# Second input phase: product P1 of the last two blocks as seven inner products, with written engine orders

## The chip, the cores and the metric

The program runs on one core of a Trainium2 chip. The metric is device time in microseconds (us) of one execution. The engines are PE (TensorE: matmuls, with their weight loads shown as PEld), DVE (VectorE), ACT (ScalarE), POOL (GpSimd) and SP (SyncE, which here only issues DMAs). Each engine works through its own list of instructions in a fixed order; waits between engines go by semaphores.

## The reference

With one layer, only the pooling mixer and the norms count:

```
h = x + pool_mixer(rms_norm(x, norm_w))          # x: (1, 4096, 1024) float32
out = rms_norm(h, final_norm_w)

def pool_mixer(h, in_w, group_w, group_b, scale, out_w):
    u, gate = split(h @ in_w, 2)                 # in_w: (1024, 2048)
    ug = u in 4 groups of 256 channels
    pooled = trailing_mean(ug[g], window 2/4/8/16) - ug
    mixed = einsum(pooled, group_w) + group_b    # 256 x 256 for each group
    return (mixed * scale * silu(gate)) @ out_w  # out_w: (1024, 1024)
```

The result must be close to float32: every float32 factor is split into a high and a low part, and each product is done as three matmul passes (high by high, high by low, low by high).

## The kernel before

**Stages.** The 4096 tokens go through three stages, in `steps`. Stage "a" (four blocks of 1024 tokens, numbered 0 to 3) makes the channels of groups 0 and 1, stage "b" (the same four blocks) those of groups 2 and 3, and stage "o" (eight blocks of 512 tokens) the output projection. The linear map of each group is folded into `in_w` at the start, so that a stage's product has 1024 output columns: 512 to be pooled and 512 of the gate.

**Seven products.** Each block's product is done as seven products of half size (Strassen's scheme in Winograd's form), P1 to P7, run in the order P1, P2, P7, P6, P5, P4, P3 (`ORDER_IN`). One such product is 48 matmuls of 512 columns. It writes four PSUM banks: P1 and P2 the banks 0 to 3 (set "x"), P7 and P4 the same banks (set "v"), P6, P5 and P3 the banks 4 to 7 (set "y"). The scheme's sums are made in PSUM and behind it:

- P1 is made in banks 0 to 3, and ACT copies it to banks 4 to 7 as the start of the "y" sum (`evict_in`, i == P1). P2 adds onto banks 0 to 3, and ACT moves the result out with a SiLU.
- P7 starts banks 0 to 3 anew; ACT moves it out (`ev["22"]`). P6 adds onto banks 4 to 7; ACT moves the sum out (`ev["21"]`), and then P5 adds onto the same banks, so **P5 may not write a bank before ACT has read it after P6**. DVE adds P5's sum to `ev["22"]`. P4 adds onto banks 0 to 3, and DVE adds that to `ev["21"]`. P3 adds onto banks 4 to 7, and ACT moves the last part out (`ev["12"]`).

**Operands.** The stage "b" operands are the sums of token blocks that stage "a" stored in DRAM (`sd`). They are loaded some steps ahead (`load_reach`) and split into high and low one step ahead (`split_in`): ACT copies the high part into an `op` tile, and DVE subtracts it to get the low part. There are four `op` tiles, 11 tiles `st` and 8 tiles `vt`. The two pools are shared by loads, evictions, pooling and the forming of weights, and a tile is handed on as soon as it is free: the next writer waits for its last reader, a DMA included.

**Inner seven.** In stage "b", for blocks 1 to 3, P7 is divided once more (`inner_in`, `split_seven`, `product_seven`): seven products of a quarter size, 84 matmuls of 256 columns in place of 48 of 512. Its weights are sums of quarters of w7, made in block 0 by `form_seven` and kept in three `st` tiles (`kept_in`, named inner). Between the inner products ACT moves 256-column cells from bank to bank (`move`), and at the end DVE adds a held cell to banks 0 and 1.

**Pooling.** When a half of a block's channels is out, `pool` does the trailing sums (on DVE, a scan of 1040 columns for each of two groups), the bias and the gate product, and stores the result to `yd`. GpSimd copies the 16 columns of history (`tails`).

**The output weights.** `load_wo` and `make_wo` form the sums of `out_w` for stage "o" in two halves: load four tiles, scale them on ACT (eight activations of 128x512), make sums on DVE and store them from SP to `wod` and `pairs_d`, the latter split into high and low. The first half is made in stage "b" at block 0's P7, the second at block 2's P6.

**Order.** A scheduler orders the instructions of each engine in stage "b", with hints (`tc.issue_after`). The wrapper `InOrder`, while it is on, makes each instruction of an engine issue behind the one before it in the program, so that the order is that of the code; before, it is on only in the later part of stage "o", and not for TensorE.

Of the kernel before, what the change touches and what calls it, by code (L numbers as in the profile page):

```python
# [10 lines left out]
F32 = mybir.dt.float32  # L11
F32R = mybir.dt.float32r
AF = mybir.ActivationFunctionType
ALU = mybir.AluOpType
# [14 lines left out]
OWN = 2  # L29
EPS = 1e-6  # L30
# [56 lines left out]
def kernel(  # L87
# [37 lines left out]
    vector, scalar, gpsimd, sync = (  # L125
        InOrder(tc, e) for e in (nc.vector, nc.scalar, nc.gpsimd, nc.sync)
# [107 lines left out]
    ]  # L234
    yd = [dram.tile([P, NK, TO], F32, name=f"yd{b}") for b in range(NBO)]
# [216 lines left out]
    def fold(q, k, g, r, ps2, pool=None, on_vector=False, midway=None):  # L452
# [3 lines left out]
        for kk in range(2):  # L456
            if kk == 1 and midway:
                midway()
            for j in range(2):
                for t in range(2):  # L460
                    for m, (a, b) in enumerate(pairs):
# [4 lines left out]
                        latest[0] = nc.tensor.matmul(  # L466
# [174 lines left out]
    def inner_in(q, b, i):  # L641

        return q == 1 and b > 0 and i == P7

    def split_in(q, b, i):
        s = xs[b]
        if inner_in(q, b, i):
            return split_seven(s)
# [16 lines left out]
    def split_seven(s):  # L665

        us = s["21"]
# [4 lines left out]
        front, back = (take("p (n k s a) -> p n k s a", n=2, k=2, s=2) for _ in range(2))  # L672
        sub(back[:, 0], a11, a21)
        sub(back[:, 1], a22, back[:, 0])
        add(front[:, 0], back[:, 1], a11)
        seven["mixed"] = sub(front[:, 1], a12, back[:, 1]).ins
        pattern = "p (s n k b a) -> p s n k b a"
        t = {}

        def sums(u, names):  # L680
# [14 lines left out]
        sums(front, (P5, P3))  # L695
        plain_op(0, {P1: 0})

        def second():
            sums(back, (P7, P6))

        def third():
            plain_op(1, {P2: 0, P4: 1})
            for u in s.pop("21"):
                give(u)
            ops[:] = [ops[n] for n in (1, 2, 0, 3)]

        seven.update(second=second, third=third)
        return t

    seven_w, kept_in, places_in = {}, [], []  # L710

    def form_seven(stage):

        if stage == 0:
            seven["raw"] = [take() for _ in range(2)]
            for h, u in enumerate(seven["raw"]):
                sync.dma_start(out=u, in_=t3d[h])
            return
        us = seven["raw"]
        if stage == 1:  # L720
            t1, t3 = (us[0][:, :, j : j + 256] for j in (256, 0))
# [6 lines left out]
            for p, (h, j) in {P1: (0, 0), P2: (1, 0), P3: (1, 1)}.items():  # L728
                c = slice(0, 256) if j else slice(256, 512)
                seven_w[p] = [w[P7][h][:, v, :, c] for v in range(2)]  # L730
            for _ in range(3):
                places_in.append(next_kept())
                kept_in.append(st.keep())
            return
        for p in ((P5, P6), (P7, P4))[stage - 2]:
            if p == P5:
                home = [w[P7][0][:, v, :, 0:256] for v in range(2)]
            else:
                t = kept_in.pop().rearrange("p v (k c) -> p v k c", k=2)
# [3 lines left out]
            seven_w[p] = home  # L743
# [4 lines left out]
    def product_seven(t, v, middle, end):  # L748
# [1304 lines left out]
```

## Time and profile before

| what | value |
|---|---|
| three runs | 907.17, 907.47, 908.05 us |
| median | 907.47 us |
| profiled execution | span 905.6 us from its first to its last instruction |
| stage "b" on PE, blocks 1 to 3 | from about 398 to 614 us |
| stage "o" on PE | from 613.7 us |

The span is that of one profiled execution; the page gives no separate device time for it. The median of the runs stands 1.9 us above the span, which is what lies ahead of the first and behind the last instruction, as far as the profiled execution was like them. The lines of the page and of the trace stand in the prediction. A row of the timeline has its start, its length, the engine, the operation with what it writes and reads, and, in brackets, how long the engine had been idle before it and who ended that.

### The profile page before, as it was taken

Reading aid. Unit: us, or ns where it says so; the run is one execution under the profiler, and the core shown is the slowest. Engines: PE = TensorE matmul, PEld = TensorE weight load, DVE = VectorE, ACT = ScalarE, POOL = GpSimd, SP = SyncE. Lnnn points to the kernel's source line nnn. Section 1 sums busy time; section 2 is a strip of 40 time slices with the busy share of each in tenths; the row PEclk is TensorE's granted clock in tenths of the full one; section 3 lists DMA queues with packets and bytes.
Section 4 is the critical chain, followed back from the end, with each engine's and each line's share of the span. In section 5 each row is a group of like instructions: output and inputs, shape, how many; then the busy total and the mean of one; then the engine's idle time right before and its main releaser. Section 6 shows DMA issues by size and latency. Waiting matters only on the chain.

```text
span 905.6 us, 12443 instructions
## 1 busy us (share of the span) xinstructions
PE 895.4 (99%) x4554; PEld 792.2 (87%) x4554; DVE 737.0 (81%) x910; ACT 519.2 (57%) x848; POOL 152.2 (17%) x250
## 2 busy tenths in 40 slices
PE   9999999999999999999999999999999999999996
PEld 7888888888888888889889888988889899998995
DVE  3899896984996996995485499698898788888798
ACT  7869547446445467446345654744557466565464
POOL 0030110110111000010100011021233343342330
PEclk9999999999999999999999999999999999999999
DMA  9989778678769475854245386699573855945953
GB/s 342 401 316 322 260 279 320 215 296 284 269 251 369 171 260 203 313 195 170 90 140 185 140 302 232 233 330 306 152 213 81 221 171 150 238 149 131 266 176 116
DMA packets 78620, 209.60 MB, mean 231 GB/s; under 512 B 7392, under 2 KB 25184, under 8 KB 77792
## 3 DMA queue, kind: packets, MB, share of 16 engines
q1 hardware_dynamic: 57872, 143.77, 45.7%
q0 software_dynamic: 19968, 63.98, 22.7%
q10 hardware_dynamic: 720, 1.06, 0.3%
q8 instruction: 35, 0.57, 0.3%
q14 instruction: 25, 0.20, 0.1%
HBM read 133.28 MB, written 75.51 MB: 231 GB/s over the span
## 4 chain that ended last, share of the span: by engine, by line
PE 88%; DVE 5%; DMA 3%; ACT 2%; issue 2%; POOL 0%; DVEq 0%; ACTq 0%; POOLq 0%; SPq 0%
PE bank L814 76%; PE bank L956 5%; PE bank L760 3%; PE bank L466 3%; DVE vt L79 2%; DVE op L79 2%; DVE st L79 1%; DMA vt<-yd 1%; DMA st<-wvd 1%; ACT vt L79 1%; DMA early<-in_group_w 0%; ACT st L79 0%; ACT op L79 0%; DMA out<-vt 0%; DVE columns L79 0%
## 5 line engine op out<-in xcount | busy, mean ns | idle before, releaser
L814 PE MATMUL bank<-op,w 128*128 128x512 f32 x2544 | 551.2, 379 | 1.5 <-ACT st L79 1.0
L814 PEld LDWEIGHTS bank<-op,w 128*128 128x128 f32 x2544 | 480.2, 189 | 70.9 <-ACT st L79 1.8
L814 PE MATMUL bank<-w,op 128*128 128x512 f32 (+1 forms) x1044 | 230.5, 377 | 0.0
L814 PEld LDWEIGHTS bank<-w,op 128*128 128x128 f32 x1044 | 192.3, 189 | 25.0
L79 DVE TENSOR_TENSOR op<-st,op 128x1024 fp32r<-128x1024 f32 x119 | 144.9, 1223 | 55.7 <-ACT op L79 55.4
L79 ACT ACTIVATE op<-st 128x1024 fp32r<-128x1024 f32 x119 | 124.8, 1052 | 81.6 <-PE bank L814 32.3
L79 ACT ACTIVATE op<-vt 128x1024 fp32r<-128x1024 f32 x66 | 69.4, 1053 | 70.0 <-DVE vt L79 41.7
L79 DVE TENSOR_TENSOR op<-vt,op 128x1024 fp32r<-128x1024 f32 x66 | 79.8, 1222 | 22.2 <-ACT op L79 22.1
L79 ACT ACTIVATE vt<-bank 128x512 f32<-128x512 f32 (+1 forms) x124 | 68.7, 577 | 46.0 <-PE bank L814 38.3
L79 DVE TENSOR_TENSOR st<-st,st 128x1024 f32<-128x1024 f32 (+2 forms) x49 | 54.8, 1134 | 30.4 <-ACT st L79 16.7
L79 ACT ACTIVATE bank<-bank 128x512 f32<-128x512 f32 (+1 forms) x84 | 41.1, 489 | 51.4 <-PE bank L814 38.6
L79 POOL COPY vt<-tails 128x32 f32<-128x32 f32 x14 | 17.5, 1257 | 271.7 <-DVE inner L79 106.8
L79 DVE TENSOR_TENSOR vt<-bank,vt 128x512 f32<-128x512 f32 (+1 forms) x92 | 52.9, 603 | 6.2 <-PE bank L956 4.6
L79 ACT ACTIVATE st<-bank 128x512 f32<-128x512 f32 (+1 forms) x60 | 34.2, 586 | 35.6 <-PE bank L814 25.0
L79 ACT ACTIVATE st<-st 128x1024 f32<-128x1024 f32 (+1 forms) x37 | 38.9, 1056 | 21.7 <-DVE st L79 19.7
L79 DVE TENSOR_TENSOR st<-bank,st 128x512 f32<-128x512 f32 (+1 forms) x70 | 42.6, 627 | 4.7 <-PE bank L956 2.5
L79 POOL DMA_DIRECT2D sd<-st x45 | 24.0, 533 | 125.7 <-DVE st L79 77.7
L956 PEld LDWEIGHTS bank<-w,op 128*128 128x128 f32 x312 | 40.4, 191 | 1.7
L956 PE MATMUL bank<-w,op 128*128 128x256 f32 x312 | 41.1, 275 | 0.0
L79 DVE TENSOR_TENSOR st<-st,vt 128x1024 f32<-128x1024 f32 (+1 forms) x33 | 38.5, 1187 | 2.8 <-DMA vt<-rd 2.8
L79 DVE TENSOR_TENSOR_SCAN vt<-vt,window 128x1040 f32<-128x1040 f32 x16 | 38.0, 2381 | 0.1
L79 DVE TENSOR_TENSOR vt<-vt 128x1024 f32<-128x1024 f32 (+3 forms) x42 | 37.7, 899 | 0.1
(119 smaller groups left out, 770.3 us busy)
## 6 DMA issues: line engine op xcount, KB each, us to landing
sd<-st POOLq DMA_DIRECT2D x45, 512.0 KB, 4.7
st<-sd SPq DMA_DIRECT2D x43, 512.0 KB, 4.7
st<-in_xt SPq DMA_DIRECT2D x28, 512.0 KB, 7.6
st<-in_x SPq DMA_DIRECT2D x21, 512.0 KB, 7.7
yd<-st SPq DMA_DIRECT2D x19, 512.0 KB, 3.0
vt<-yd SPq DMA_DIRECT2D x17, 512.0 KB, 10.7
out<-vt POOLq DMA_DIRECT2D x16, 512.0 KB, 3.3
st<-yd SPq DMA_DIRECT2D x15, 512.0 KB, 8.0
```

The source lines that it names most:

```text
L79: r = f(*args, **kwargs)
L466: latest[0] = nc.tensor.matmul(ps, a[:, kk, 2 * j + t, :], maps, start=t + m == 0, stop=t == 1 and m == len(pairs) - 1,).ins
L760: latest[0] = nc.tensor.matmul(cell(n, c).rearrange("p (a s) -> p a s", s=2), x1, x2, start=i == P1 and k + m == 0, stop=k == 1 and m == 2 ...
L814: latest[0] = nc.tensor.matmul(ps, a, b, start=start and n == 0, stop=stop and n == 2, skip_group_check=True).ins
L956: latest[0] = nc.tensor.matmul(ps, x1, x2, start=start and k + n == 0, stop=k == 1 and n == 2, skip_group_check=True,).ins
```

## The change

In blocks 2 and 3 of stage "b" (`STEADY = 2`), P1 also is done as seven inner products. Its weights need three more tiles' worth of inner sums than SBUF keeps, so the three `inner` tiles now hold one set at a time: both sets are stored to DRAM (`store_set`, from GpSimd, in block 1) and loaded in turn from SP (`load_set`: P7's set behind each P1, P1's set behind block 2's P7). The sums of P1's weights are made in block 1, from freshly loaded and scaled rows of `in_w` (`form_seven(P1, ...)`, four more activations of 128x512). The second half of the output weights is made in block 1 in place of block 2 (`load_wo(1)` at P2, `make_wo(1)` at P7).

For blocks 2 and 3 all engines follow the code's order (`InOrder.on`, now for TensorE too), which `steady_in` writes out: where each split, eviction and pooling step stands. Pooling is a generator (`pool_group`) that goes on by one, two or three stages at a time, and DVE copies the histories there. P3's eviction is put off into the next block's P1. Block 3's last steps load and split the output weights by `load_late_w` and `split_late_w`.

```diff
+STEADY = 2
     def inner_in(q, b, i):
-        return q == 1 and b > 0 and i == P7
+        return q == 1 and (i == P7 and b > 0 or i == P1 and b >= STEADY)
...
+    def store_set(i):
+        for place, t in zip(set_d[i], kept_in):
+            gpsimd.dma_start(out=place, in_=t.bitcast(F32))
+
+    def load_set(i):
+        for place, t in zip(set_d[i], kept_in):
+            sync.dma_start(out=t.bitcast(F32), in_=place)
...
+            else:
+                seven["raw"] = [load_rows(in_w, 2 * h, D + H) for h in range(2)]
             return
         us = seven["raw"]
         if stage == 1:
+            if i == P1:
+                for h, u in enumerate(us):
+                    scale_rows(u, pair(norm_c, h, 0))
...
+    def steady_in(n):
+        _, b, i = steps[n]
+        sets, s, final = sets_of("b", b), xs[b], b == NB - 1
+        x_banks, y_banks = sets["x"], sets["y"]
+        if i == P1:
+            halves = late["halves"] = []
+            def first_half():
+                pool_stages(1)
+                halves.append(split_half(s["12"][0]))
...
+            product_seven(
+                P1, split_up.pop(n), x_banks, first_half, [evict_last((0, 1)), evict_last((2, 3))]
+            )
+            late.pop("12", None)
+            for c in range(4):
+                evicted[0] = copy(y_banks[c], x_banks[c]).ins
+            load_set(P7)
+        elif i == P2:
+            seven_in = seven_parts(s, "21")
+            seven_in["sums"]()
+            late["halves"].append(split_half(s["12"][1]))
...
+            product_in(P2, late.pop("halves"), sets, False)
+            seven_in["second"]()
+            pool_stages(2)
...
+            pool_stages({P6: 2, P5: 3, P4: 0, P3: 3}[i])
+            if i == P4 and not final:
+                late["next"] = seven_parts(xs[b + 1], "11")
+                late["next"]["sums"]()
+            product_in(i, split_up.pop(n), sets, False)
...
+        if kind == "b" and b == STEADY - 1:
+            if i == P1:
+                store_set(P7)
+            elif i in forming_seven[:3]:
+                with tc.issue_after(latest_split[0]), tc.issue_after(latest_copy[0]):
+                    for stage in {P7: (0,), P6: (1,), P5: (2, 3)}[i]:
+                        form_seven(P1, stage)
+                if i == P5:
+                    store_set(P1)
...
-            if (kind, b, i) in (("b", 0, P2), ("b", 2, P7)):
-                load_wo(b // 2)
-            if (kind, b, i) in (("b", 0, P7), ("b", 2, P6)):
+            if (kind, i) == ("b", P2) and b < 2:
+                load_wo(b)
+            if (kind, i) == ("b", P7) and b < 2:
                 with tc.issue_after(evicted[0]):
-                    make_wo(b // 2)
+                    make_wo(b)
```

**How the lists move, place 1: ACT in block 1, from P7's last eviction on.** ACT's list before, from the row that moves P7's bank 3 out (`bank3_72` is bank 3, and so on; `op` rows are the high parts of operands; the rows that read bank 4 to 7 move P6's sum out):

```order
L79 ACTIVATE vt2_102<-bank3_72 128x512
L79 ACTIVATE op1_86<-st9_98 128x1024
L79 ACTIVATE op3_88<-st5_94 128x1024
L79 ACTIVATE vt3_103<-bank4_73 128x512
L79 ACTIVATE vt3_103<-bank5_74 128x512
L79 ACTIVATE st4_93<-bank6_75 128x512
L79 ACTIVATE st4_93<-bank7_76 128x512
```

ACT's list after the change, from the same eviction of bank 3 (the rows with `colt` scale rows of `out_w` and `in_w`, `x2` is two instructions; `w1_0` is the first of P1's new weight sums):

```order
L80 ACTIVATE vt3_103<-bank3_72 128x512
L80 ACTIVATE st5_94<-st5_94,colt_114 128x512 x2
L80 ACTIVATE vt6_106<-vt6_106,colt_114 128x512 x2
L80 ACTIVATE vt5_105<-vt5_105,colt_114 128x512 x2
L80 ACTIVATE vt0_100<-vt0_100,colt_114 128x512 x2
L80 ACTIVATE st4_93<-st4_93,colt_114 128x512 x2
L80 ACTIVATE vt2_102<-vt2_102,colt_114 128x512 x2
L80 ACTIVATE op3_88<-st1_90 128x1024
L80 ACTIVATE op0_85<-st8_97 128x1024
L80 ACTIVATE w1_0_77<-st4_93 128x2x256
L80 ACTIVATE vt5_105<-bank4_73 128x512
L80 ACTIVATE vt5_105<-bank5_74 128x512
```

Before P6's bank 4 is moved out there now stand twelve scalings, two operand copies and one weight copy, where two operand copies stood. Right behind those rows ACT's list goes on with the weight copies and the other two banks (`st6_95` is one tile that is written, stored by SP, and written again):

```order
L80 ACTIVATE inner2_2750<-st4_93 128x512
L80 ACTIVATE st6_95<-st3_92 128x1024
L80 ACTIVATE st5_94<-vt6_106 128x1024
L80 ACTIVATE inner10_2749<-vt2_102 128x512
L80 ACTIVATE inner0_2751<-vt2_102 128x512
L80 ACTIVATE st6_95<-vt0_100 128x1024
L80 ACTIVATE tails_116<-vt4_104 128x32
L80 ACTIVATE st6_95<-bank6_75 128x512
L80 ACTIVATE st6_95<-bank7_76 128x512
```

The eviction of banks 6 and 7 now goes into a tile that twice before held a high part on its way to DRAM, so it stands behind two stores.

**Place 2: PE in block 1, P5 and P4.** PE's list before, behind P6's last row (`w5` is P5's weight, `w4` P4's; `x6` is six matmuls):

```order
L814 MATMUL bank4_73<-op3_88,w5_0_609 128x512 x6
L814 MATMUL bank5_74<-op3_88,w5_0_609 128x512 x6
L814 MATMUL bank6_75<-op3_88,w5_0_609 128x512 x6
L814 MATMUL bank7_76<-op3_88,w5_0_609 128x512 x6
L814 MATMUL bank4_73<-op1_86,w5_1_610 128x512 x6
```

PE's list after the change, from the same place:

```order
L80 MATMUL bank0_69<-op3_88,w4_0_704 128x512
L80 MATMUL bank1_70<-op3_88,w4_0_704 128x512
L80 MATMUL bank2_71<-op3_88,w4_0_704 128x512
L80 MATMUL bank3_72<-op3_88,w4_0_704 128x512
L80 MATMUL bank4_73<-op2_87,w5_0_615 128x512 x6
L80 MATMUL bank5_74<-op2_87,w5_0_615 128x512 x6
L80 MATMUL bank4_73<-op1_86,w5_1_616 128x512 x6
L80 MATMUL bank5_74<-op1_86,w5_1_616 128x512 x6
L80 MATMUL bank0_69<-op3_88,w4_0_704 128x512 x5
```

The scheduler draws parts of P4 ahead of P5: first four single matmuls of P4, then P5 on banks 4 and 5, then 30 matmuls of P4 (of which the last row shown is the start), and only then P5 on banks 6 and 7.

**Place 3: ACT in block 2, P1.** ACT's list before, where P1's four banks are copied as the start of the "y" sum:

```order
L79 ACTIVATE bank4_73<-bank0_69 128x512
L79 ACTIVATE bank5_74<-bank1_70 128x512
L79 ACTIVATE bank6_75<-bank2_71 128x512
L79 ACTIVATE op0_85<-st7_96 128x1024
L79 ACTIVATE bank7_76<-bank3_72 128x512
```

ACT's list after the change, for the same product:

```order
L80 ACTIVATE bank2_71<-bank0_69 128x256
L80 ACTIVATE st5_94<-bank0_69 128x256
L80 ACTIVATE bank3_72<-bank1_70 128x256
L80 ACTIVATE st5_94<-bank1_70 128x256
L80 ACTIVATE bank2_71<-bank0_69 128x256
L80 ACTIVATE op0_85<-st1_90 128x1024
L80 ACTIVATE bank3_72<-bank1_70 128x256
L80 ACTIVATE bank0_69<-bank2_71 128x256
L80 ACTIVATE bank1_70<-bank3_72 128x256
L80 ACTIVATE bank4_73<-bank0_69 128x512
L80 ACTIVATE bank5_74<-bank1_70 128x512
L80 ACTIVATE bank6_75<-bank2_71 128x512
```

Eight moves of 256 columns now stand ahead of the four copies, and the copy of bank 0 comes behind the last move and behind DVE's addition to bank 0.

More of the change, by code (lines that the diff above doesn't have):

```diff
@@ L234 @@
     ]
+    set_d = {
+        i: [dram.tile([P, 2, H], F32, name=f"set{i}_{n}") for n in range(3)] for i in (P1, P7)
+    }
     yd = [dram.tile([P, NK, TO], F32, name=f"yd{b}") for b in range(NBO)]
@@ L788, in product_seven @@
             move(3, 2, c)
+        for f in between[1:2]:
+            f()
         for c in range(2):
@@ L1115, with pool_stages @@
+    stages = deque()
+    def pool_stages(count):
+        while stages and count:
+            if next(stages[0], "end") == "end":
+                stages.popleft()
+            count -= 1
     ev, evicted, copied = {}, [None], []
```

299 lines of the change are left out of this document (210 added, 89 removed).

## The prediction

> **What bounds the kernel now.** I first read the page's busy times and the chain of work that ended last.
>
> ```profile
> span 905.6 us, 12443 instructions
> PE 895.4 (99%) x4554; PEld 792.2 (87%) x4554; DVE 737.0 (81%) x910; ACT 519.2 (57%) x848; POOL 152.2 (17%) x250
> PE 88%; DVE 5%; DMA 3%; ACT 2%; issue 2%; POOL 0%; DVEq 0%; ACTq 0%; POOLq 0%; SPq 0%
> ```
>
> PE is busy for 99% of the span and makes 88% of the chain. A busy PE need not be at its peak, so the next view is PE's timeline over stage "b", where a bracket would show idle time.
>
> ```profile
> 367.82 4.80 PE L814 MATMUL bank<-op,w 128*128 128x512 f32 x21 [0.55 <-ACT st L79]
> 373.13 46.02 PE L814 MATMUL bank<-op,w 128*128 128x512 f32 x212 [0.51 <-DVE op L79]
> ...
> 428.59 62.33 PE L814 MATMUL bank<-op,w 128*128 128x512 f32 x288
> ```
>
> The last idle time of PE in this stage stands at 373 us, in block 0. From there to the end of block 3 no row has a bracket. So blocks 1 to 3 are bound by the count and length of the matmuls alone; nothing that the other engines do there can gain anything, and all that they do late will cost. The windows by stage (busy time of PE, PEld, DVE, ACT, POOL; granted clock; DMA share) say how much cover is left:
>
> ```profile
> 428.59:438.95 10.36, 10.36 (x50) 9.08 (x49) 4.25 (x5) 5.67 (x9) 0.00 (x0) 1.00 0.46 151
> ...
> 470.00:541.90 71.90, 71.90 (x374) 64.07 (x374) 49.87 (x50) 40.12 (x61) 4.85 (x4) 1.00 0.55 198
> 541.90:613.70 71.80, 71.80 (x374) 63.96 (x373) 60.82 (x65) 41.13 (x58) 8.99 (x9) 1.00 0.75 259
> ```
>
> The first row is P6 of block 1, the other two are blocks 2 and 3. The clock is full. DVE has 22 us free in block 2 and 11 in block 3, ACT some 30 in each: on average there is room for more of both.
>
> **Term 1: the matmuls.** The chain in order of time gives both kinds of product:
>
> ```profile
> 490.92 9.60 PE bank L760 x84
> 500.52 62.16 PE bank L814 x288
> ```
>
> 288 matmuls of 512 columns are six plain products, so one takes 62.16 / 6 = 10.36 us, or 215.8 ns for a matmul. The inner seven take 9.60 us, or 114.3 ns for one of 256 columns. That is 6.4 ns more than half of 215.8, so an eighth fewer columns shortens the product by 7% only. P1 of blocks 2 and 3 changes from the one to the other: 2 x (10.36 - 9.60) = **1.52 us less**. As PE had no idle time there, this is also the most that the change can give in its place.
>
> [...]
>
> **Term 2: ACT in block 1.** Here work is added where there was just enough room. In program order, ACT after P7 of block 1 has the two evictions and operand copies that it had, and then twelve scalings ahead of P6's evictions (place 1 of the order). Their prices:
>
> ```profile
> 427.45 1.07 ACT L79 ACTIVATE op<-vt 128x1024 fp32r<-128x1024 f32 x1
> 428.42 2.04 ACT L79 ACTIVATE vt<-bank 128x512 f32<-128x512 f32 x4
> 430.33 1.08 ACT L79 ACTIVATE op<-st 128x1024 fp32r<-128x1024 f32 x1
> 435.27 0.60 ACT L79 ACTIVATE vt<-bank 128x512 f32<-128x512 f32 x1 [0.24 <-PE bank L814]
> ...
> 511.41 4.99 ACT L79 ACTIVATE st<-st,colt 128x512 f32<-128x512 f32 x8
> ...
> 408.70 2.91 SPq L79 DMA_DIRECT2D yd<-vt  x2
> ...
> st<-in_in_w SPq DMA_DIRECT2D x5, 512.0 KB, 7.0
> ...
> L79 DVE TENSOR_TENSOR st<-st,st 128x1024 f32<-128x1024 f32 (+2 forms) x49 | 54.8, 1134 | 30.4 <-ACT st L79 16.7
> ```
>
> Up to 428.42 nothing on ACT is changed. Four evictions (2.04) and one operand copy (1.0, the distance of such rows in a queue) end at 431.46. Twelve scalings at 4.99 / 8 = 0.62 are 7.5 and end at 438.96. Then come the high parts of two operands (1.05, 1.0), the first of P1's weight sums (512 columns, about as an eviction, 0.55) and the eviction of bank 4 (0.55): 440.0 for the first operand, **442.1 for bank 4**. Before, bank 4 was out at 435.9. The loads for the scalings stand on SP beside the two stores of 408.7 and behind operand splits that ended by 422; at up to 7.0 us each they land before ACT comes to them.
>
> PE ends P6 at 438.95 (first of the windows above). Its list now has four single matmuls of P4 (place 2), for which the operand is ready at 440.0: idle 1.1. They take 4 x 0.216 = 0.9, to 440.95; P5 on bank 4 then waits for 442.15: idle 1.2. So PE loses **2.2 us**. What is hidden: P5's operands and the low parts from DVE (started at 436.4 by the scaled rows, sums at 1.1 or about half that, P4's low part at 444) are all ready before PE comes to them (447). Block 0 shows the same pattern in small, in the two brackets above: there `make_wo(0)` also stands at P7, with eight scalings and with P7 as a plain product, and PE lost 0.55 + 0.51. Bounds: 0, if the scalings moved behind the evictions (the list excludes it), and 5.
>
> **Term 3: the tile that is stored twice.** The eviction of bank 6 in block 1 now writes `st6`, which holds two high parts in turn, each stored by SP. ACT's first copy into it ends at 443.8; store, copy (1.05), store, eviction (0.6) end at 445.45 + 2L, with L the time of a store.
>
> ```profile
> sd<-st POOLq DMA_DIRECT2D x45, 512.0 KB, 4.7
> st<-sd SPq DMA_DIRECT2D x43, 512.0 KB, 4.7
> ...
> pair<-st SPq DMA_DIRECT2D x10, 512.0 KB, 3.4
> ```
>
> With the 3.4 us of the same stores before, bank 6 is out at 452.3. PE needs it at 442.15 + 24 x 0.2158 (P5 on banks 4 and 5) + 30 x 0.2158 (P4) = 453.8. I take **0**, with 1.5 us to spare; the end of the range is L = 4.7, which gives 454.9 and costs 1.1, and 5.5, which costs 2.7. A gain is excluded, as PE had no idle time there.
>
> **Term 4: the written order in blocks 2 and 3.** P1 gets the chain of moves that P7 has, between ACT and PE (place 3). P7 of block 1 shows it fitting, without a bracket on PE:
>
> ```profile
> 426.06 0.37 ACT L79 ACTIVATE bank<-bank 128x256 f32<-128x256 f32 x1 [0.41 <-PE bank L760]
> 426.74 0.70 DVE L79 TENSOR_TENSOR bank<-bank,vt 128x512 f32<-128x512 f32 x1 [0.89 <-PE bank L760]
> ...
> 401.06 0.58 ACT L79 ACTIVATE bank<-bank 128x512 f32<-128x512 f32 x1 [0.93 <-PE bank L814]
> ...
> L79 DVE TENSOR_TENSOR op<-st,op 128x1024 fp32r<-128x1024 f32 x119 | 144.9, 1223 | 55.7 <-ACT op L79 55.4
> ...
> L79 DVE TENSOR_TENSOR_SCAN vt<-vt,window 128x1040 f32<-128x1040 f32 x16 | 38.0, 2381 | 0.1
> ```
>
> New against P7: P2 accumulates onto the same banks, so it must wait until DVE has added the held cell to bank 0 and ACT has copied the bank (0.58, as in P1 before). In P7's times that is 427.44 + 0.6 = 428.0, and the next product starts at 428.59: 0.5 us to spare; bank 1 comes 1.3 us later. Ahead of this addition DVE has in P1 a scan and an operand's low part, which by their rows (2.4 and 1.2) end about 0.8 us before it is needed. On DVE a block gains four sums at 0.6, two operand splits at 1.2 and two additions at 0.7, about 6 us against 22 and 11 free; block 2 loses the eight scalings and their sums. The loads of the inner sets (three of 512 KB on SP, 4.7 us each by the row above, issued as each tile comes free, the last with P1's end) have P2's 10.4 us and 2.7 us of P7 before they are read. Behind them on SP stand loads that are used 20 us and more later. The output weights' splits of block 3 are the same number as before. I take **0**; where the cover is gone it costs what DVE is late, between 0 and 1 us for each of the two P1, so 0 to 2. Stage "o" has the same list on PE as before: 0.
>
> **Sum.** The profiled execution: 905.6 - 1.5 + 2.2 = 906.3 us. The runs' median stands 1.9 above that span, and I take the same distance: **908.2 us**. A measurement of this kernel can tell about 0.2% from no change, so "same" is 905.7 to 909.3.
>
> [...] The scalings by themselves, in the grouped view (busy, mean ns of one):
>
> ```profile
> L79 ACT ACTIVATE st<-st,colt 128x512 f32<-128x512 f32 x8 | 5.0, 707 | 0.0
> ```
>
> [...]
>
> **Rivals.**
>
> 1. *The forecast*, PE idle 1 to 3.5 us in block 1 and nowhere else new: 907.0 to 909.3. For it speaks the list, which is fixed, and block 0's brackets. Chance 0.50.
> 2. *Only the count shows.* PE loses less than 1 us in block 1, since the scalings run more tightly than 0.62 us or the operand is ready early: 906.0 to 906.9, in the limit 907.47 - 1.52 = 905.95. Against it: 12 scalings would have to take less than 6.3 us. A gain of over 0.2% would need more than the 1.52 us that there is, say that a bracket in block 0 goes too. Chance 0.14, of which 0.03 below 905.7.
> 3. *The stores decide: slower.* The place is ACT's wait for `st6` in block 1. The price is 2 x (L - 4.1) us: from L = 4.1 on PE waits for bank 6, and ACT, which stands still, moves nothing else. At L = 4.7 to 5.5 it is 909.3 to 910.9. For it: ten stores within about 12 us, beside the loads for block 2, and loads and stores of this size at 4.7 in the median elsewhere. Against it: 3.4 for these stores before, ten of them in a row too. Chance 0.24.
> 4. *The strict order in blocks 2 and 3 holds PE up* at P1's hand-over to P2 or at a set that comes late: 0.5 to 1 us for each P1, on top of the forecast, so 909 to 910.5. For it: the 0.5 to 0.8 us to spare, and a DVE list that can no longer be passed by a late scan. Against it: P7 runs through with the same moves. Chance 0.12.
>
> **How the numbers follow.** Faster holds 0.03 (from 2). Same holds the forecast (0.50), the rest of 2 (0.11) and the near ends of 3 and 4 (0.04): 0.65. Slower is what is left of 3 and 4: 0.32. The range leaves out 2 in 10: below 906.0 lies about 0.06, above 911.0 (L beyond 5.5, or 3 and 4 together) about 0.1.
>
> **What would show it.** In the profile after: the 84 rows of P1 at 9.6 us in blocks 2 and 3 (term 1); two brackets on PE at about 440 and 442 us, released by ACT (term 2), 2.2 us together; none, or a small one, at 454 (term 3); none between 475 and 612 (term 4). The forecast is wrong if PE's idle time in block 1 is over 3.5 us, if brackets stand at the start of P2 or P7 in blocks 2 and 3, or if stage "o" starts later than 614.4 (613.7 - 1.5 + 2.2).

## The result and the profile after

| kernel | median | runs | profiled span |
|---|---|---|---|
| before | 907.76 us | 907.17 to 908.48 (4) | 905.6 us |
| after | 917.54 us | 916.75 to 917.97 (4) | 915.0 us |

The change made the kernel slower by 1.1%: ratio 1.011, 95% interval 1.0095 to 1.0124. The forecast was 908.2, with a range from 906.0 to 911.0.

The page of the changed kernel, its span and the busy time of each engine:

```profile
span 915.0 us, 12691 instructions
PE 895.7 (98%) x4626; PEld 793.4 (87%) x4626; DVE 757.3 (83%) x946; ACT 529.5 (58%) x870; POOL 143.1 (16%) x250
```

PE is busy as long as before (895.7 against 895.4), though twice an eighth of a product's columns went: the 1.5 us that this saves come back as work at half clock (0.77 + 0.73 us, counted below). The span is 9.4 us longer, so the rest of the loss is waiting. PE's timeline of the changed kernel has the waits as brackets (the shortest ones only as a row that is too long); from P6 in block 1 of stage "b" on:

```profile
428.27 10.53 PE L80 MATMUL bank<-op,w 128*128 128x512 f32 x48
439.42 1.13 PE L80 MATMUL bank<-op,w 128*128 128x512 f32 x4 [0.61 <-ACT op L80]
441.36 11.92 PE L80 MATMUL bank<-op,w 128*128 128x512 f32 x54 [0.81 <-ACT vt L80]
453.75 21.51 PE L80 MATMUL bank<-op,w 128*128 128x512 f32 x110 [0.47 <-ACT st L80]
...
479.23 1.90 PE L80 MATMUL bank<-op,w 128*128 128x256 f32 x12
...
551.02 1.60 PE L80 MATMUL bank<-op,w 128*128 128x256 f32 x12 [0.34 <-ACT bank L80]
...
615.21 52.78 PE L80 MATMUL bank<-w,op 128*128 128x512 f32 x246
...
670.50 2.75 PE L80 MATMUL bank<-w,op 128*128 128x512 f32 x12
679.91 1.65 PE L80 MATMUL bank<-inner,op 128*128 128x256 f32 x6 [6.65 <-DVE vt L80]
681.35 21.70 PE L80 MATMUL bank<-w,op 128*128 128x512 f32 x108
```

A bracket leaves out the run-out of the matmul before it (0.17 us at 438.8: the row of 428.27 is 10.53 us long, where 48 matmuls are followed after 10.36), so the price of a wait is better counted from start to start, with 0.2158 us for a matmul of 512 columns (288 in 62.16 us before). 48 matmuls from 428.27 end at 438.63: 0.79 us lost by 439.42. In the same way 1.08 are lost by 441.36, 0.74 by 453.75 and 6.82 by 679.91. The row of 479.23 takes 0.28 more than the 1.62 of its kind, and 0.50 are lost at 551.02. The row of 679.91 is followed after 1.44 us, where six matmuls of 256 columns are followed after 0.67 elsewhere, and the 108 matmuls behind it take 0.73 us more than the same 108 one block later. The windows of the changed kernel (length; busy PE, PEld, DVE, ACT, POOL; granted clock; DMA share, GB/s) say why:

```profile
675.00:676.00 1.00, 0.00 (x0) 0.00 (x0) 0.74 (x2) 0.05 (x1) 0.82 (x1) 1.00 1.07 233
676.00:677.00 1.00, 0.00 (x0) 0.00 (x0) 1.00 (x2) 0.90 (x2) 0.00 (x0) 0.50 1.10 231
...
682.00:683.00 1.00, 1.00 (x4) 0.79 (x4) 1.00 (x3) 0.00 (x0) 0.00 (x0) 0.59 0.71 250
683.00:684.00 1.00, 1.00 (x6) 0.89 (x5) 0.85 (x3) 0.00 (x0) 0.00 (x0) 1.00 0.04 12
```

While PE waited, its granted clock fell from 1.00 to 0.50 at 676.0, 2.7 us after PE stood still (673.26), and stayed there until 682.8 (from the 0.59 of that row), 2.9 us after PE had gone on at 679.91. So the one wait costs 6.82 + 0.77 + 0.73 = **8.3 us**. Against the kernel before:

| part | us |
|---|---|
| ahead of block 1's P6 (starts 0.3 us earlier) | -0.3 |
| P1 of blocks 2 and 3, by the count | -1.5 |
| block 1, waits at 439 and 441 | +1.9 |
| block 1, wait at 454 | +0.7 |
| P1 of blocks 2 and 3, waits | +0.8 |
| stage "o", wait at 673 and half clock | +8.3 |
| sum; the last matmul ends at 907.63 against 898.03 | +9.9; +9.6 |

The 0.3 us between the two sums are a short wait that the kernel before has in stage "o" (its six matmuls at 666.15 are followed after 0.96 us in place of 0.67) and the changed kernel has not.

What ends the long wait is in the chain of waits of the changed kernel:

```profile
664.36 3.06 DMA out<-st
667.43 7.68 DMA st<-wod
...
679.91 198.89 PE bank L80 x1128
```

A row of the output must be stored before the second half of the raw w7 can be loaded, and DVE waits for that load to form the sums of the own weights (SP's rows, then DVE's, of the changed kernel):

```profile
648.12 0.32 SPq L80 DMA_DIRECT2D vt<-wod  x1
...
667.43 0.32 SPq L80 DMA_DIRECT2D st<-wod  x1
```

```profile
675.23 0.69 DVE L80 TENSOR_TENSOR st<-st,vt 128x512 f32<-128x512 f32 x1 [4.72 <-DMA st<-wod]
```

In the kernel before both halves had been loaded early:

```profile
639.10 6.06 SPq L79 DMA_DIRECT2D vt<-wod  x2
```

The lists, which are fixed before any run, say what moved. SP's two loads of the raw w7, and of POOL's four stores of output rows of block 0 the third and fourth, before:

```
L79 DMA vt5_105<-wod7_0_129 128x1024
L79 DMA vt2_102<-wod7_1_130 128x1024
...
L79 DMA out_0<-st7_96 128x1024
L79 DMA out_0<-vt0_100 128x1024
```

and the loads and the third store after:

```
L80 DMA vt6_106<-wod7_0_129 128x1024
L80 DMA st10_4410<-wod7_1_130 128x1024
...
L80 DMA out_0<-st10_4410 128x1024
```

`take` hands out the tile that has been free longest. The changed order of takes and gives in stage "b" changed which free tiles were the oldest when the raw w7 was loaded: two `vt` before, one `vt` and `st10` after. The program had given `st10` back when it issued the store of the third output row, but the load still had to wait until that store had landed: the store ended at 667.42, and the load was issued at 667.43. Before, the third row's tile (`st7`) went to one of the three own weights instead.

### The profile page after: what moved, and what is told of

Its sections match the earlier page's. It is cut to its first block, busy times and chain, and to the rows that moved or that the text cites. A ratio compares the mean times of both kernels' runs of the same rounds, so it can differ in the third digit from the quotient of the medians.

```text
span 915.0 us, 12691 instructions
## 1 busy us (share of the span) xinstructions
PE 895.7 (98%) x4626; PEld 793.4 (87%) x4626; DVE 757.3 (83%) x946; ACT 529.5 (58%) x870; POOL 143.1 (16%) x250
## 4 chain that ended last, share of the span: by engine, by line
PE 84%; DVE 6%; ACT 4%; DMA 2%; issue 2%; POOL 0%; SPq 0%; DVEq 0%; ACTq 0%; POOLq 0%
PE bank L80 84%; DVE vt L80 2%; DVE st L80 2%; ACT st L80 1%; DVE op L80 1%; DMA st<-wod 1%; DMA early<-in_wut 1%; ACT bank L80 1%; ACT vt L80 1%; DMA pair<-st 1%; DMA out<-st 0%; ACT w L80 0%; DVE columns L80 0%; ACT op L80 0%; PE bank L536 0%
## 5 line engine op out<-in xcount | busy, mean ns | idle before, releaser
L80 PE MATMUL bank<-op,w 128*128 128x512 f32 (+1 forms) x2688 | 561.3, 370 | 3.4 <-ACT st L80 1.0
L80 PEld LDWEIGHTS bank<-op,w 128*128 128x128 f32 x2688 | 490.8, 189 | 71.6 <-ACT st L80 1.8
L80 PE MATMUL bank<-w,op 128*128 128x512 f32 (+1 forms) x1356 | 264.1, 354 | 0.0
L80 DVE TENSOR_TENSOR vt<-bank,vt 128x512 f32<-128x512 f32 (+1 forms) x106 | 60.3, 595 | 12.6 <-PE bank L80 11.1
L80 DVE TENSOR_TENSOR st<-st,st 128x1024 f32<-128x1024 f32 (+2 forms) x40 | 41.9, 1072 | 20.7 <-DMA st<-wvd 12.5
L80 ACT ACTIVATE st<-st 128x1024 f32<-128x1024 f32 (+2 forms) x39 | 40.0, 1032 | 18.8 <-DVE st L80 17.9
L80 PE MATMUL bank<-inner,op 128*128 128x256 f32 x234 | 32.3, 279 | 6.6 <-DVE vt L80 6.6
L80 DVE TENSOR_TENSOR st<-bank,st 128x512 f32<-128x512 f32 (+1 forms) x56 | 34.4, 633 | 3.5 <-PE bank L80 3.5
L80 PEld LDWEIGHTS bank<-inner,op 128*128 128x128 f32 x234 | 30.1, 195 | 7.9 <-DVE vt L80 7.0
L80 POOL DMA_DIRECT2D vt<-in_x x30 | 27.0, 952 | 50.7 <-issue 22.3
```

The source lines that it names most:

```text
L80: r = f(*args, **kwargs)
```

## The experiments

The theory: (A) the loss in stage "o" is that tile; block 1's loss is the output weights that now stand there. The rivals: the written order and the late loads of weights hold stage "o" up (B), or the clock dips by itself (C). Each median stands beside the kernel before on the same chip.

| run | median (range; runs) | before | ratio, 95% interval |
|---|---|---|---|
| e1_tile_aside | 911.19 (909.84 to 912.17; 6) | 907.63 | 1.0037, 1.0024 to 1.0050 |
| e2_before_row | 916.42 (915.19 to 918.35; 4) | 907.63 | 1.0098, 1.0082 to 1.0113 |
| e3_wo_03_12 | 923.26 (922.55 to 923.77; 4) | 907.63 | 1.0170, 1.0155 to 1.0186 |
| e4_seven_p5 | 912.97 (912.81 to 913.14; 2) | 907.63 | 1.0058, 1.0037 to 1.0078 |
| e5_row_last | 911.36 (910.53 to 912.29; 4) | 907.48 | 1.0039, 1.0026 to 1.0053 |
| e6_both | 910.21 (908.96 to 912.43; 11) | 907.48 | 1.0029, 1.0020 to 1.0038 |
| e7_both12 | 909.68 (908.55 to 911.28; 4) | 907.48 | 1.0020, 1.0006 to 1.0035 |
| e8_reuse | 910.32 (910.21 to 913.08; 5) | 907.27 | 1.0037, 1.0020 to 1.0054 |
| e9_reuse_beh | 911.69 (910.35 to 913.41; 4) | 907.27 | 1.0047, 1.0032 to 1.0063 |
| e10_wo_block2 | 911.45 (910.69 to 913.47; 6) | 907.27 | 1.0047, 1.0035 to 1.0060 |
| e11_less_dve | 909.62 (909.06 to 911.68; 10) | 907.65 | 1.0027, 1.0018 to 1.0036 |
| e12_best | 906.78 (905.99 to 908.48; 11) | 907.65 | 0.9988, 0.9979 to 0.9997 |

### The tile, taken away and put in

`e1_tile_aside`, against the changed kernel:

```diff
+        if (kind, b, i) == ("o", 1, P1):
+            aside.append(st.take(...))
...
-        raws[i] = {"held": [take() for _ in range(2)]}
+        raws[i] = {"held": [take() for _ in range(2 - len(aside))] + aside[:]}
```

> The changed kernel, with one tile set aside: at the first step of block 1 of stage "o" an st tile that has long been free (st1) is reserved for the second half of the raw w7, in place of st10, whose rows of the output are still on their way out. Nothing else is changed; every matmul and every written order stays. Theory A (the tile: the load waits for the store of an output row): the load is issued at about 648 with the first half, PE's idle time at 673 us (6.8 us) and the half-clock stretch behind it (1.5 us lost) go, 917.5 - 8.3 = 909.2 us, range 908.6 to 910. Rival B (the weights that blocks 2 and 3 now load and split late, or the written order, hold stage "o" up): the own products' operands come late with any tile; PE's idle time stays at 3 us or more, 913 us or more. Rival C (the clock dips by itself): the idle time goes, a half-clock stretch of 6.8 us stays somewhere in stage "o", about 910.7 us.

`e2_before_row`, against the kernel before:

```diff
-        raws[i] = {"held": [take() for _ in range(2)]}
+        raws[i] = {"held": [take()]}
+        if i == P7:
+            vt.free.rotate(-1)
+        raws[i]["held"].append(take(pool=vt if i == P7 else None))
+        if i == P7:
+            vt.free.rotate(1)
```

> The kernel before, with one tile exchanged: the second half of the raw w7 goes into the tile vt0, which held a row of the output (its second row, stored a little later than the one in the changed kernel), in place of vt2. No inner P1, no written order in blocks 2 and 3, no late weights. Theory A (the tile): the load is issued behind that store, PE idles about 6 to 8 us at about 671 us, and the clock falls to 0.5 behind it for 1 to 2 us lost: 907.8 + 7 to 10 = 914.5 to 918 us. Rival B (written order or late weights): nothing of that is here, 907.2 to 908.6 us. Rival C (the clock dips by itself): idle time but no half-clock stretch, 913 to 916 us.

e2 has none of the change but the wait, and it lost 8.8 us. PE's timeline and DVE's of e2:

```profile
677.73 1.65 PE L961 MATMUL bank<-inner,op 128*128 128x256 f32 x6 [5.87 <-DVE vt L79]
679.17 4.43 PE L814 MATMUL bank<-w,op 128*128 128x512 f32 x12
```

```profile
673.17 0.69 DVE L79 TENSOR_TENSOR vt<-vt,vt 128x512 f32<-128x512 f32 x1 [6.19 <-DMA vt<-wod]
```

The 12 matmuls from 679.17 take 4.26 us to the next row at 683.43, where 2.59 is usual: the granted clock of e2 is at half there too, from 675.7 to 682.5 us. e1 has all of the change but the wait: neither the long bracket nor a half-clock stretch ahead of the end is left (mean granted clock 0.998 in its profile, 0.994 in that of the changed kernel). Together they show A for the long wait; B and C fall. e1 missed its number, though: 9.8 us above the kernel before became 3.6, so 6.2 us came back, not 8.3. In the profiles stage "o" is 7.1 us shorter than in the changed kernel (285.4 against 292.4 us from its first matmul to its last). The rest is a wait of 0.56 us for an operand from DVE in P1 of block 2, where all lists are still those of the changed kernel, and two short waits that are new (PE's timeline, then ACT's, of e1):

```profile
670.59 0.38 PE L80 MATMUL bank<-inner,op 128*128 128x256 f32 x1 [0.40 <-ACT inner L80]
671.32 0.82 PE L80 MATMUL bank<-inner,op 128*128 128x256 f32 x5 [0.35 <-DVE inner L80]
```

```profile
669.91 0.63 ACT L80 ACTIVATE inner<-vt 128x512 fp32r<-128x512 f32 x1 [0.91 <-DMA out<-st]
```

The same tile, given to the first own weight in place of the load, still waited for the same store, 0.91 us on ACT. So e5 took it last, and e8 went round it:

```diff
 # e5_row_last, against e1
             aside.append(st.take(...))
+            st.free.rotate(1)
 # e8_reuse, against the changed kernel; end_weights(P2)
-        for u in raws.pop(i)["held"]:
-            give(u)
+        us = raws.pop(i)["held"]
+        aside.append(us[0])
+        give(us[1])
 # and load_inner as in e1
```

> The kernel of e1_tile_aside, with the three tiles that become own weights taken in another order: the tile that held a row of the output (st10) is now written last of the three, not first. Theory A (every use of that tile waits for the store of the row): the two short idle times of PE at 670.6 and 671.3 us in e1_tile_aside (0.4 and 0.35) go, nothing else changes: 911.0 - 0.75 = 910.2 us, range 909.4 to 911. Rival B (they come from DVE's list, which is fuller there than before): they stay, 911 us.

> The changed kernel, with one edit: the second half of the raw w7 is loaded into the tile that held the first half of the raw w2 (st3, whose last reader is DVE at about 659 us), in place of st10; the three tiles that become own weights stay st1, st6 and st8 as in the changed kernel. So neither a load nor a weight waits for the two rows of the output that are stored at 664 us and later. Theory A (the tile): the load is issued at about 659.5 and lands before DVE needs it at 670; PE has no idle time over 0.3 us in stage "o" and the clock no half stretch: 917.5 - 8.3 = 909.2 us, range 908.6 to 910. Rival B (e1 and e5 kept 0.75 and 1.8 us of idle time there since DVE or ACT are late anyway): 1 us or more stays, 910 to 911.5 us.

Both missed, and e8's rival B held: the two short waits went, and another one of 1.8 (e5) and 1.4 us (e8) stood behind them. In e8 (PE's timeline):

```profile
674.78 0.94 PE L80 MATMUL bank<-inner,op 128*128 128x256 f32 x6 [1.42 <-DVE st L80]
```

No load or store stands in the chain of waits that ends here, back to 636 us; in the changed kernel this wait probably lay within the 6.65, which no run shows by itself. The windows of the first 26.3 us of stage "o", before and in e8 (DVE is the third engine), name a suspect:

```profile
613.70:640.00 26.30, 26.30 (x123) 23.04 (x122) 21.34 (x23) 10.08 (x14) 5.86 (x7) 1.00 1.01 294
```

```profile
615.50:641.80 26.30, 26.30 (x124) 23.03 (x123) 26.19 (x27) 13.26 (x19) 5.91 (x7) 1.00 0.99 301
```

DVE comes out of stage "b" with more left to do: it is busy for 26.2 of 26.3 us where it had 21.3. e11 leaves eight of its instructions out:

```diff
-        for j in range(2):
+        for j in range(0 if q and b == NB - 1 else 2):
             vector.scalar_tensor_tensor(
```

> The kernel of e8_reuse with DVE work left out: for block 3 the bias and the product with the gate (eight DVE instructions of about 0.7 us, most of them in the first 26 us of stage "o") are not done, so the last 1024 rows of channels 512 to 1023 go on without them. Theory A (what is left in stage "o", 1.4 us idle at 675, is DVE's backlog: it is busy for 26.2 of the first 26.3 us of the stage, where it had 21.3 in the kernel before): DVE is ahead by 3 to 5 us, the idle time falls below 0.3 us, e8 - 1.4 = 908.9 us, range 908.2 to 909.6. Rival B (the chain through the norm of the output rows, ACT, POOL and a semaphore each, sets that time): it stays at 1 us or more, 909.8 to 910.6 us.

```profile
615.50:641.80 26.30, 26.30 (x123) 23.03 (x123) 22.40 (x21) 13.25 (x19) 5.89 (x7) 1.00 0.96 278
```

```profile
673.81 0.94 PE L80 MATMUL bank<-inner,op 128*128 128x256 f32 x6 [0.38 <-DVE st L80]
```

With 3.8 us less on DVE the wait falls from 1.42 to 0.38 us. DVE's timeline of e11 shows how: DVE is done early and stands idle for an operand from ACT, while in e8 it has no idle time from 606 to 645 us and begins the next sum (`st<-st`) at 640.13 in place of 639.17, and all that follows on it is about 1.0 us later.

```profile
638.03 1.23 DVE L80 TENSOR_TENSOR op<-st,op 128x1024 fp32r<-128x1024 f32 x1 [3.75 <-ACT op L80]
```

So DVE's backlog causes 1.0 us of this wait; what the other 0.4 waits for stays open. Beside the kernel before on its own chip e11 stands 2.0 us above it, e8 3.0 us, and the runs scatter over more than the 1.0 us that it moved; e11's median, 909.62, lies between the two forecasts (up to 909.6, and from 909.8).

### Block 1

`e4_seven_p5`, `e6_both` and `e7_both12`, against e1, e5 and e5:

```diff
 # e4 and e6
-                    for stage in {P7: (0,), P6: (1,), P5: (2, 3)}[i]:
+                    for stage in {P7: (0,), P6: (), P5: (1, 2, 3)}[i]:
 # e6 and e7, in evict_in, i == P6
+            if q and b == STEADY - 1:
+                vt.free.rotate(1)
+                st.free.rotate(1)
+                ev["21"] = [take(pool=vt), take(pool=st)]
```

> The kernel of e1_tile_aside, with the four scalings of P1's weights and their sums asked for one step later (at P5 of block 1, not P6); the eight scalings of the output weights stay at P7. Theory A (twelve scalings in a row are the idle time): ACT's list loses 2.5 us ahead of P6's bank 4, so the two idle times at 439 and 441 go and only the one at 453 (0.7 us, the tile that is stored twice) stays: 907.4 us, range 906.8 to 908. Rival B (the eight alone suffice, or the tile of the eviction waits for a store): 908.4 to 909.6 us.

> The kernel of e5_row_last with block 1 mended: the four scalings of P1's weights at P5 (as in e4_seven_p5), and P6's sum moved out into two tiles that hold nothing on its way to DRAM (vt1, st9) in place of vt5 and st6. Theory A (ACT's twelve scalings and the stores of the eviction's tiles are the idle time in block 1): PE has no idle time from 431 to 470, 2.6 to 2.9 us come back: 910.2 - 2.9 = 907.3 us, range 906.5 to 908.2. What is left against 907.6 - 1.5 = 906.1 are the waits within P1 of blocks 2 and 3 (0.3 to 0.6 and 0.5 us). Rival B (DVE's weight sums and operand splits are as late as ACT): idle time of 1 us or more stays, 908.3 us or more.

> As e6_both, but with the four scalings of P1's weights at P6 as in the changed kernel: all twelve scalings stay, only the tiles of P6's eviction change. Theory A (with the tiles free, ACT's order can put the evictions ahead, so the twelve scalings alone cost nothing or little): idle at 439 to 442 below 1 us and none at 454, 907.3 to 908.5 us. Rival B (the scalings' order decides): two idle times as before, 1.9 us, none at 454: 909.2 us.

All three missed the time of their theory A. In e4 the waits at 439 and 441 are gone, but not since bank 4 is out earlier: nine scalings still stand ahead of it, and ACT begins to move it out 12.18 us after P6's start (441.50 against 429.32), where the changed kernel took 12.45. The operand of P4 is copied behind eight scalings in place of twelve, and the scheduler put ten matmuls of P4 ahead of P5 in place of four, which fills the time until bank 4 is out. The third wait grew from 0.47 to 2.72, and e4 is 1.8 us slower than e1. PE's timeline and ACT's of e4:

```profile
429.32 25.82 PE L80 MATMUL bank<-op,w 128*128 128x512 f32 x117
457.86 2.43 PE L80 MATMUL bank<-op,w 128*128 128x512 f32 x10 [2.72 <-ACT st L80]
```

```profile
457.21 1.09 ACT L80 ACTIVATE st<-bank 128x512 f32<-128x512 f32 x2 [2.75 <-DMA pair<-st]
```

So the tile that is stored twice is a wait by itself, as rival 3 of the prediction had it. e6 and e7 evict into other tiles, and all three waits go. In e7 all twelve scalings still stand ahead of bank 4; but with `vt1` in place of `vt5` the scheduler puts the eviction right behind them, ahead of the two operand copies and the weight copy, and P5 ahead of P4 on PE. Bank 4 begins to leave at 438.38, 0.3 us ahead of P6's end. ACT's rows of the changed kernel, then of e7:

```profile
440.72 1.07 ACT L80 ACTIVATE vt<-bank 128x512 f32<-128x512 f32 x2
```

```profile
438.38 1.07 ACT L80 ACTIVATE vt<-bank 128x512 f32<-128x512 f32 x2
```

So the twelve scalings alone don't make the waits at 439 and 441; they do it together with the three copies ahead of the eviction and with P4 ahead of P5. But in e6 and e7 the operands of P3 come late, from loads on SP behind the stores of the pairs and from DVE, in e6:

```profile
461.18 13.44 PE L80 MATMUL bank<-op,w 128*128 128x512 f32 x71 [1.50 <-DVE op L80]
```

(0.78 in e7, and another 0.91 in P1 of block 2). Counted from the first row of P7 in block 1 that reads `inner` to the first such row of P1 in block 2, e10 below takes 51.05 us, the changed kernel 53.74, e6 53.16 and e7 53.96: the loss of 2.7 us moved, and most or all of it stayed. The medians of e6 and e7 stand 1.2 and 1.7 us below e5's, but hardly by block 1: e5's profile has a wait of 0.96 us in P1 of block 2 that the changed kernel, with the same lists up to there, has not.

The next two move the output weights out of this place. `e3_wo_03_12`, against e1, loads them at P3 of block 0 and forms them at P2 of block 1; `e10_wo_block2` puts them back into block 2 (on top of e9):

```diff
 # e3
+            if (kind, b, i) in (("b", 0, P2), ("b", 0, P3)):
+                load_wo(int((b, i) != (0, P2)))
+            if (kind, b, i) in (("b", 0, P7), ("b", 1, P2)):
...
+                    make_wo(int((b, i) != (0, P7)))
 # e10
+            if (kind, b, i) in (("b", 0, P2), ("b", 2, P2)):
+                load_wo(b // 2)
...
+            if (kind, b) == ("b", 2) and i in (P7, P6, P5, P4):
+                next(parts_wo, None)
```

> The kernel of e1_tile_aside, and the second half of the output weights is loaded at P3 of block 0 and formed at P2 of block 1, in place of P2 and P7 of block 1. The four scalings of P1's weights stay at P6. Theory A (the eight scalings ahead of P6's evictions are the idle time in block 1, and the stores of their tiles the idle time at 453): PE's three idle times in block 1, 2.6 us counted from one matmul's start to the next, go; 909.2 - 2.6 = 906.6 us, range 905.9 to 907.4. Rival B (P1's weight sums alone fill ACT and DVE there): half of it or less goes, 908 to 909.2 us. Rival C (the eight scalings hold up P2's evictions or P7's operands instead): new idle time of 1 us or more between 405 and 430, 908 us or more.

> The kernel of e9_reuse_beh, with the second half of the output weights back in block 2, where the kernel before made it: loaded at P2, scaled behind P7's evictions, its sums and stores given out over P6, P5 and P4 in the written order. Block 1 is left with the four scalings of P1's weights. Theory A (the output weights in block 1 are what PE waits for there: the scalings at 439 and 441, the stores at 454): PE has no idle time from 428 to 470; blocks 2 and 3 have room for it on ACT and DVE; what is left of the change is the saving by the count: 907.5 - 1.5 = 906.0 us, range 905.4 to 907. Rival B (the written order leaves no room in block 2): idle time of 1 to 4 us there, 907 to 910 us.

e3 lost 12 us more than e1. PE's timeline and ACT's of e3:

```profile
434.41 1.65 PE L80 MATMUL bank<-op,inner 128*128 128x256 f32 x6 [13.04 <-ACT vt L80]
```

```profile
433.98 0.38 ACT L80 ACTIVATE vt<-bank 128x256 f32<-128x256 f32 x1 [2.80 <-DMA pair<-vt]
```

P7's held cell got the tile of a high part that was still to be formed and stored: the mechanism of stage "o" once more, at another place. e3 missed by it. None of the three waits of block 1 is left in e3. In e10 PE has no bracket from 428.79 to 544.9 (one row of 216 matmuls runs from there through block 1), so the output weights are what block 1 loses by. But e10 missed too, and is as slow as e9 (911.45 against 911.69), since the time went elsewhere: P1 of block 3 waits 0.41 us behind ACT's

```profile
544.47 0.38 ACT L80 ACTIVATE st<-bank 128x256 f32<-128x256 f32 x1 [0.91 <-DMA pair<-st]
```

which is a held cell again, in the tile of the last pair, and then 1.39 us for the low part of an operand. DVE makes that right behind the pooling (its row ahead of it ends at 545.49), so it is DVE's list that is late there:

```profile
545.40 1.22 DVE L80 TENSOR_TENSOR op<-st,op 128x1024 fp32r<-128x1024 f32 x1
```

### P1's own waits, and all together

`e9_reuse_beh`, against e8:

```diff
-                P1, split_up.pop(n), x_banks, first_half, [evict_last((0, 1)), evict_last((2, 3))]
+                P1, split_up.pop(n), x_banks, first_half, [list, evict_last((0, 1, 2, 3))]
```

> The kernel of e8_reuse, and in P1 of blocks 2 and 3 the four evictions of the block before stand behind all of ACT's moves between the banks, where two of them stood ahead of the last pair of moves. Theory A (PE's waits at 479 and 551 us are the last moves, which come behind those evictions on ACT): the 0.3 and 0.5 us go, e8 - 0.8 = 908.4 us. Rival B (they wait for the operand that ACT copies in between): they stay, and the copies of the banks at the end of P1 come 1.1 us later, as e8 or up to 1 us more.

The wait at 551 went, and one of 0.19 at 554 came for it; the row of 479 is as long as before (1.90 us, at 479.62). The medians (911.69 against 910.32, ranges that overlap) don't separate e9 from e8: inconclusive.

`e12_best`, against e10:

```diff
+        highs = [take() for _ in range(3)]
+        for p, high in zip((P5, P4, P3), highs):
...
-            pool_stages({P6: 2, P5: 3, P4: 0, P3: 3}[i])
+            pool_stages({P6: 3, P5: 4, P4: 0, P3: 1}[i] if final else {P6: 2, P5: 3, P4: 0, P3: 3}[i])
```

> All that helped in one kernel, as a candidate: the changed kernel with the raw w7 in the tile of the raw w2 (e8), the evictions behind the moves (e9), the second half of the output weights in block 2 (e10; its last three pairs now at P5, with three tiles for the high parts, so that P1 of block 3 does not write a tile that is still being stored), and the pooling of block 2 a few steps earlier in block 3. Theory A (the added waits are the tiles, block 1 and DVE's backlog): no idle time in block 1 nor at 545 to 547, 0.5 to 1.5 us left at 675: 907.3 - 1.5 + 0.4 + 1 = 907.2 us, range 906.2 to 908.5, so at best 0.1% below the kernel before. Rival B (DVE's work in stage "b" is too much with the inner sums and cannot be placed anywhere without a wait): 909 us or more.

```profile
374.98 48.70 PE L80 MATMUL bank<-op,w 128*128 128x512 f32 x236 [0.51 <-DVE op L80]
...
553.26 13.31 PE L80 MATMUL bank<-op,w 128*128 128x512 f32 x72 [0.19 <-ACT bank L80]
...
673.05 0.94 PE L80 MATMUL bank<-inner,op 128*128 128x256 f32 x6 [0.37 <-DVE st L80]
```

Those three are PE's brackets from 374 us to the end in e12. It changes several things at once, so it shows that the waits can be taken away together, not what each edit is worth. The time lies inside its range. It is 10.8 us faster than the changed kernel and 0.87 us faster than the kernel before; the interval, 0.9979 to 0.9997, lies below 1, by a difference that is smaller than the scatter of the runs. That is a little over half of the 1.5 us of the count. Its DVE is busy for 65.0 of 71.9 us in block 3 (542.0 to 613.9 us), so there is little room for more.

## Why the prediction was wrong

- **What bounds the kernel** was right for stage "b": PE is saturated there, and each new wait in block 1 and in P1 of block 3 cost at least its bracket (0.61, 0.81, 0.47 and 0.34 us against 0.79, 1.08, 0.74 and 0.50 counted from start to start). The views were not read beyond it, although PE is as full in stage "o".
- **Term 1**, -1.5 us: right. P1 of block 3 starts at 543.70 (192 matmuls of 512 columns from 502.27) and P2 at 553.80; less the 0.50 of its wait that is 9.6 us.
- **Term 2**, 2.2 us in two brackets at 440 and 442 by ACT: the places, the releaser and nearly the size were right, 1.9 us at 439.4 and 441.4. The sum followed the lists, and the lists decide; the twelve scalings that it named are a part of the cause only. e7 keeps them and has neither wait, since its list moves bank 4 out right behind them. e10 shows the output weights as the work that made the list so.
- **Term 3**, 0 with 1.5 us to spare: mis-sized, 0.7 us, and 2.7 in e4. I had taken the median of the stores before, 3.4 us. The median hardly changed (3.3 us), but the one store that PE waits behind took 4.85 in the chain of the changed kernel. Bank 6 was out at 453.7, 1.4 us after the 452.3 of the sum; that alone would have fitted the 1.5 us to spare, but PE also came for the bank 0.8 us earlier than in the sum (453.0 against 453.8).

```profile
448.17 4.85 DMA pair<-st
453.10 0.61 ACT st L80
```

- **Term 4**, 0 with a bound of 2: the waits within P1 were 0.8 us, inside the bound. "On DVE a block gains ... about 6 us against 22 and 11 free" counted free time as an average. DVE did not find the place within the blocks: in the first 26.3 us of stage "o" it was busy 4.8 us longer than before (26.2 against 21.3), of which taking 3.8 away won 1.0 us back (e8, e11).
- **The step that failed** is the last sentence of term 4: "Stage "o" has the same list on PE as before: 0." The list was the same, but not what its rows wait for. The change reorders takes and gives in stage "b"; with that, tiles rotate through all that comes after, and SP's list of the changed kernel showed the load of w7 in a tile that POOL's list was about to store from. e1 and e2 put the price of that one tile at 6.2 us taken away and 8.8 us put in, where the term had 0. The prediction followed one such tile (`st6` in term 3) and looked for no other.
- **The rivals.** The slower case had a mechanism of the right kind, a tile that is still being stored, in block 1 and at 3 us at most. The mark that was set, a start of stage "o" after 614.4, was passed by 0.8 us (615.21): terms 3 and 4 added 1.5, and the 0.3 us of term 2 and the earlier start took some of it away. The other 8 us lay behind it, in a stage for which no mark was set.

## What to carry to other kernels

Where tiles are handed out by age, a change in the order of takes and gives changes which buffer each later load gets, in stages that the change does not touch. So compare the DMA queues' lists over the whole program for loads whose tile has a store pending; reserve a clean tile for loads that PE waits for, since one exchanged tile moved these kernels by 6.2 to 8.8 us. And the free time of an engine as an average over a stage did not say here where work fits: DVE had 22 and 11 us free in blocks 2 and 3 before, and with the change it was busy 4.8 us longer in the first 26.3 us of stage "o". Look for what an engine still owes at a stage's end.

## What the runs showed of the hardware

- **The granted clock fell to half behind three long waits of PE.** It fell 2.7 us after PE stood still in the changed kernel (6.65 us idle), 3.8 us in e2 (5.87 us idle) and 2.1 us in e3 (13.0 us idle), and not in e4 (2.72 us idle, mean clock 0.997). It stayed low until 2.9 us after PE went on in the changed kernel, 4.8 us in e2 and 6.1 us in e3, so for 6.8, 6.8 and 17.1 us in all. In the changed kernel the wait thus cost 8.3 us where its bracket has 6.65. The windows of e3 put the half clock from 423.4 to 440.5:

```profile
423.00:424.00 1.00, 0.00 (x0) 0.00 (x0) 0.00 (x0) 1.00 (x3) 0.00 (x0) 0.72 1.04 418
...
440.00:441.00 1.00, 1.00 (x9) 1.00 (x9) 0.00 (x0) 0.37 (x1) 0.00 (x0) 0.75 0.97 256
```

  What sets these delays and lengths was not shown.
- **Waits of PE varied between runs of the same instructions.** Stage "a" has a wait at 223 us, behind a load of `wvd` that took 8.66 us in the profile of the kernel before and 10.8 in that of e12. The wait was absent in the profile of the changed kernel, 0.43 us before and 1.98 in e12; so e12's profile lost 1.55 us more there than that of the kernel before, and 1.98 more than that of the changed kernel, ahead of all that was changed. In P1 of block 2 the changed kernel, e1 and e5, with the same lists up to there, waited 0, 0.56 and 0.96 us for DVE.

```profile
224.89 144.23 PE L80 MATMUL bank<-op,w 128*128 128x512 f32 x667 [1.98 <-ACT st L80]
```
